# Layer 1 expert weights: partitions that hold neighbouring rows

## The chip, the cores and the metric

The kernel runs on one core of a Trainium2 chip. The metric is the device time of one execution in microseconds (us). The engines are PE (TensorE matmul; its weight loads are shown as PEld), DVE (VectorE), ACT (ScalarE), POOL (GpSimd) and SP (SyncE, which here only issues transfers); 16 DMA engines move data between HBM and the on-chip memory of 128 partitions.

## The reference, cut to what matters

Two layers of a hybrid model over 256 latent and 256 context tokens, model width 1024, all in float32. Each layer has a mixer (layer 0: SSD heads and a convolution; layer 1: a gated linear recurrence) and behind it a mixture of 16 experts, of which the router gives each token two. The change is in the experts of layer 1, which only the 256 latent tokens pass. With t the tokens (256 x 1024) and combine the weight of each token for each expert:

```
def expert(acc, p):
    wg, wu, wd, gate_col = p           # 1024x512, 1024x512, 512x1024
    y = (silu(t @ wg) * (t @ wu)) @ wd
    return acc + gate_col[:, None] * y, None
out, _ = lax.scan(expert, zeros, (w_gate, w_up, w_down, combine.T))
```

The sum over the 1024 rows of wg and wu, and over the 512 rows of wd, may be taken in any order, so long as each row meets its own channel of the token or of the hidden layer.

## The kernel before, in words

**The weights' stream.** All large weights come through one object, `S` (class Stream, lines 28 to 87). `S.add` enters a transfer in a plan, in the order of use; `fill` (line 62) takes a free buffer from the rings and issues the next transfer of the plan on SP's queue (line 76). `S.done` gives a buffer back and calls `fill`. A buffer is 128 partitions x 8 KB, a transfer 1 MB. The order on SP's queue is thus the plan's, and a transfer starts when the one before it is issued and a buffer is free. Layer 1's experts stand last in the plan (`plan_moe(1)`, line 218): for each expert gate and up of the first 512 rows, gate and up of the second 512 rows, and then the two halves of the down weights of the expert before.

**How a transfer lays out rows.** `rows` (line 206) lays rows r0 to r0 + 128n so that partition p holds rows r0 + p, r0 + 128 + p and so on: `(k p) c -> p k c`. For gate and up n is 4 and a row is 512 f32 (2 KB); for layer 1's down weights n is 2 and a row is 1024 f32 (4 KB). One piece of HBM that follows on is one row.

**The experts of layer 1** (lines 2530 to 2720). The work is written out in order by hand, one expert after the other, with no planner. For a pair of experts `slots1` finds the up to 64 tokens of each, and `gather1` (line 2584) collects their channels with matmuls: the stationary operand is a block of 128 tokens x 128 channels of the normalised tokens `h[t]`, the moving one a one-hot matrix of 128 tokens x 2 x 64 slots, and the result, in PSUM, has 128 channels on the partitions and the slots in the free dimension. `mm` is the helper at line 98 (its call at 99), so all these matmuls have line L99. Block 4 kh + k holds the channels of the rows that weight buffer kh holds in its k-th part. One f32 matmul is two loads and two matmuls in the trace, so a gather (2 x 4 x 2 calls) has 32.

`hidden_half` multiplies the gathered columns with gate and up, side by side in the two halves of the array. `hidden` (line 2606) takes silu and product, turns the 64 x 512 hidden values with four PE transposes (line 2615, data as the stationary operand) so that 128 hidden channels lie on the partitions, and `down1` (line 2621) multiplies these with the down weights. `add1` adds the result back to the tokens' rows in PSUM. Per pass of the loop over e, PE's order is: gate and up of e, down of e - 1, the transposes of e, adding back e - 2, and for every even e the slots and the gather of the next pair. Two experts are one gather.

```
h = [xg_hu[t].rearrange("p (k c) -> p k c", k=8) for t in range(2)]     # L2562
mm(pv[:, k], h[t][:, 4 * kh + k], oh[:, t, 0:n, 0].bitcast(F32), ...)   # L2593
PE.transpose(p[:, CAP * c:CAP * c + CAP], s_[up, 128 * c:128 * c + 128], ident[up, up])   # L2615
```

A branch at line 2731 holds a loop for experts with more than 64 tokens; its own loads are at line 2743.

Of the kernel before, what the change touches and what calls it, by code (L numbers as in the profile page):

```python
# [6 lines left out]
F32 = mybir.dt.float32  # L7
# [9 lines left out]
D = 1024  # L17
# [72 lines left out]
def build(tc, I, out):  # L90
# [4 lines left out]
    PE, DV, SC, GP, SY = nc.tensor, nc.vector, nc.scalar, nc.gpsimd, nc.sync  # L95


    def mm(o, l, r, start=True, stop=True):
        PE.matmul(o, l, r, start=start, stop=stop, skip_group_check=True)  # L99
# [17 lines left out]
    def ps_tr():  # L117
        return ps.tile([128, 512], F32, name="tr", tag="tr", bufs=2)

    def ps_y(shape=(128, 512)):  # L120
        return ps.tile(list(shape), F32, name="y", tag="y", bufs=2)
# [82 lines left out]
    S = Stream(nc)  # L204

    def rows(ap, r0, n, c0, w):
        return ap[r0:r0 + 128 * n, c0:c0 + w].rearrange("(k p) c -> p k c", p=128)

    w_in = I["ab_w_in"][0]
    w_out = I["ab_w_out"][0]  # L210
    hw_in = I["hg_w_in"][0]
# [6 lines left out]
    def plan_moe(l):  # L218
        def down(e):
            for hf in range(2):  # L220
                if l:
                    S.add(("d", l, e, hf), rows(I["moe_w_down"][l, e], 256 * hf, 2, 0, D))
                else:
                    S.add(("d", l, e, hf), rows(I["moe_w_down"][l, e], 0, 4, 512 * hf, 512))
        gu = (("g", "moe_w_gate"), ("u", "moe_w_up"))
        for e in range(NEXP):
            for (n, w), kh in [(x, kh) for kh in range(2) for x in gu] if l else [(x, kh) for x in gu for kh in range(2)]:
                S.add((n, l, e, kh), rows(I[w][l, e], 512 * kh, 4, 0, 512))
            if e:
                down(e - 1)  # L230
        down(NEXP - 1)
# [39 lines left out]
    for b in MOD_ROUTE:  # L271
        plan_mod(1, b)
    plan_moe(0)
    for b in MOD_TAIL:
        plan_mod(1, b)
# [17 lines left out]
    for kh in range(2):  # L293
        for hf in range(2):
            S.add(("ho", hf, kh), rows(hw_out, 512 * kh, 4, 512 * hf, 512))
    plan_moe(1)


# [17 lines left out]
    def unit(pool, name, dt=F32):  # L316

        return pool.tile([128, 2048], dt, name=name, tag=name, bufs=1)
# [57 lines left out]
    def mask(name, op, dt=F32):  # L376
        t = const.tile([128, 128], dt, name=name)
        DV.tensor_scalar(t, jp, 0.0, None, op0=op)
        return t

    ident = mask("ident", ALU.is_equal)
# [96 lines left out]
    class Pieces:  # L478
# [26 lines left out]
        def next(self, keep=False):  # L505

            if not keep:
                self.release()
            self.ahead()
            v, r, b = self.ready.pop(self.pos)  # L510
            self.pos += 1
            self.held.append((r, b))
            return v
# [57 lines left out]
    def quarter(u, i):  # L571

        return u[i // 4][:, 512 * (i % 4):512 * (i % 4) + 512]
# [632 lines left out]
    oh, ol = ([quarter(uo, 8 * j + c) for c in range(8)] for j in range(2))  # L1206
# [1193 lines left out]
    for hb in range(2):  # L2400
        lb = LB.main()
        for j, i in enumerate((4, 2)):
            p = PS.main()
# [26 lines left out]
        for d in range(2):  # L2430
            if d:
                q = QS.main()
# [50 lines left out]
    xg_hu = [hu[3][:, D * t:D * t + D] for t in range(2)]  # L2483
# [18 lines left out]
    for kh in range(2):  # L2502
# [3 lines left out]
        for hf in range(2):  # L2506
            for i in range(2):
                wh, wl = next_piece()
                for a in range(2):
                    for q in range(2):  # L2510
                        k = 4 * kh + 2 * i + q
                        l, r = tail["oth"][:, k, 128 * a:128 * a + 128], tail["otl"][:, k, 128 * a:128 * a + 128]
# [11 lines left out]
    T, CAP = 256, 64  # L2524
# [3 lines left out]
    def mt(name, shape, bufs=1, dt=F32):  # L2528
        return mp.tile(list(shape), dt, name=name, tag=name, bufs=bufs)

    def pair_tile():
        return mt("oneh", [128, 2, 2, 2, CAP], 2, F32R)

    def which(oh, rank):

        for i in range(rank.shape[2]):
            DV.tensor_tensor(oh[:, :, i], bc(iot[:, None, None, 0:CAP], [128, 2, 2, CAP]),
                             bc(rank[:, :, i][:, :, None, None], [128, 2, 2, CAP]), op=ALU.is_equal)
# [20 lines left out]
    pc = route([0, 0], mt, bt, rv, vb, False, ps_tr,  # L2559
               (lambda: row_half(0), lambda: row_half(1), lambda: which(OH[0], rv[:, :, 0, 0:2].bitcast(F32))))  # L2560
    S.ring([rows_s], last=moe_last[1])
    h = [xg_hu[t].rearrange("p (k c) -> p k c", k=8) for t in range(2)]  # L2562
    gh, itok = (hp.tile([128, n], F32, name=m, tag=m, bufs=1) for m, n in (("masksr", 512), ("masks", T)))
    GP.iota(itok, pattern=[[1, T]], base=0, channel_multiplier=0, allow_small_or_imprecise_dtypes=True)
    fg = [wp.tile([128, 512], F32, name="fg", tag="tmp", bufs=2) for _ in range(2)]
# [4 lines left out]
    def slots1(oh, cols):  # L2570

        n = len(cols)
        p = ps_tr()
        for i, col in enumerate(cols):
            for t in range(2):
                mm(p[:, 4 * i:4 * i + 4], oh[:, t, i].rearrange("p c l -> p (c l)"), col[:, t], t == 0, t == 1)
        yield
        tw = mt("tw", [128, 2, 2], 4)
        pv = p[:, 0:4 * n].rearrange("p (i c) -> p i c", i=n)
        DV.tensor_scalar(tw[:, 0:n, 0], pv[:, :, 1], BIG, None, op0=ALU.add)  # L2580
        DV.tensor_reduce(tw[:, 0:n, 1], pv[:, :, 2:4], axis=AX.X, op=ALU.add)
        yield tw

    def gather1(oh, n):

        n_x[0] += 1
        x = xy[:, 1024 * (n_x[0] % 2):1024 * (n_x[0] % 2) + 8 * n * CAP].rearrange("p (k i l) -> p k i l", k=8, i=n)
        for kh in range(2):
            p = ps_tr()
            pv = p[:, 0:4 * n * CAP].rearrange("p (k i l) -> p k i l", k=4, i=n)  # L2590
            for k in range(4):
                for t in range(2):
                    mm(pv[:, k], h[t][:, 4 * kh + k], oh[:, t, 0:n, 0].bitcast(F32), k == 0 and t == 0, t == 1)  # L2593
                if k % 2:
                    yield
            SC.activation(x[:, 4 * kh:4 * kh + 4], pv, AF.Copy)
            yield None if kh else x

    def hidden_half(acc, x, wg, wu, kh):

        for k in range(4):
            for c, w in enumerate((wg, wu)):
                mm(acc[CAP * c:CAP * c + CAP], x[:, 4 * kh + k], w[:, k], kh == 0 and k == 0, kh == 1 and k == 3)
            yield

    def hidden(acc):

        s_, up = mt("sg", [128, 512]), slice(CAP, 2 * CAP)
        SC.activation(s_[up], acc[0:CAP], AF.Silu)  # L2609
        DV.tensor_tensor(s_[up], s_[up], acc[up], op=ALU.mult)  # L2610
        for _ in range(4):
            yield
        p = ps_tr()
        for c in range(4):
            PE.transpose(p[:, CAP * c:CAP * c + CAP], s_[up, 128 * c:128 * c + 128], ident[up, up])  # L2615
        yield
        a = mt("hT", [128, 4, CAP], 2)
        SC.activation(a.rearrange("p c l -> p (c l)"), p[:, 0:4 * CAP], AF.Copy)
        yield a
# [23 lines left out]
    def add1(z, back, last):  # L2643

        for t in range(2):
            for hf in range(2):
                mm(res[t][hf], back[:, 128 * t:128 * t + 128], z[hf], False, last)
# [19 lines left out]
    def gather_of(q):  # L2667
        v = last_of(gather1(OH[q], 2))
        XT1.update({2 * q + i: v[:, :, i] for i in range(2)})
# [61 lines left out]
    with tc.If(most > CAP):  # L2731
        rvD = dram.tile([128, 8, 16], F32, name="rvD1")
        SY.dma_start(rvD[:, :, :], rv.bitcast(F32).rearrange("p t i e -> p (t i) e"))
        wov = [unit(hw, f"hu{i}") for i in (7, 8)]
        with tc.For_i(0, NEXP, 1) as e:
            col, colr = mt("col", [128, 2, 4]), mt("colr", [128, 2, 4], dt=F32R)
            SY.dma_start(col.rearrange("p t (i o) -> p (t i) o", o=1), rvD[:, :, bass.ds(e, 1)])
            DV.tensor_copy(colr, col)

            def weights(w, r0, n):  # L2740
                nw[0] += 1
                t = wov[nw[0] % 2].rearrange("p (k c) -> p k c", k=n)
                SY.dma_start(t, I[w][1][bass.ds(e, 1), r0:r0 + 128 * n, :].rearrange("o (k p) c -> p (o k) c", p=128))
                return t

            for b in range(1, T // CAP):
                DV.tensor_scalar(col[:, :, 0], col[:, :, 0], -float(CAP), None, op0=ALU.add)
                oh = pair_tile()
                which(oh, col[:, :, 0:1])
                *_, tw = slots1(oh, [colr])  # L2750
                tw = tw[:, 0]
                x = next(v for v in list(gather1(oh, 1)) if v is not None)[:, :, 0]
                acc = ps_y()
                for kh in range(2):
                    for _ in hidden_half(acc, x, *(weights(w, 512 * kh, 4) for w in ("moe_w_gate", "moe_w_up")), kh):
                        pass
                *_, a = hidden(acc)
                *_, v = down1(a, [weights("moe_w_down", 256 * kh, 2) for kh in range(2)], tw)
                add1(*v, True)
# [13 lines left out]
    for t in range(2):  # L2773
        for hf in range(2):
            o = XL[:, t][:, 512 * hf:512 * hf + 512]
# [41 lines left out]
```

## Time and profile before

| | |
|---|---|
| median of 3 runs | 1571.52 us (1570.26 to 1576.47) |
| profiled execution | 1573.54 us, span 1571.7 us |
| PE busy | 1402.3 us, 89% |
| weight loads (PEld) | 940.1 us, 60% |
| DVE, ACT, POOL busy | 59%, 48%, 41% |
| mean granted TensorE clock | 0.953 of full speed |
| DMA over the span | 337.67 MB, 215 GB/s, 181,687 packets |

How to read it: the page divides the span into 40 slices, gives the costliest groups of instructions, and follows the chain of work that ended last back from the end. Shares over the span are means over stages with different limits, so the stage of layer 1's experts is read by itself, with windows, the chain in order of time, the waits, and groups by line and shape. In a group the operation stands as out<-in, then its shapes, its count, its busy time in us and the mean ns of one. For a matmul `tr<-oneh,hu 128*128 128x128`, the first input is the moving operand, the second the stationary one, and 128*128 is the stationary operand's size. Loads and matmuls overlap, so the busy time of a group is less than count times mean.

### The profile page before, as it was taken

How to read it: one execution, taken by the hardware profiler on the slowest of the kernel's cores; microseconds unless marked ns; L12 is line 12 of the kernel's file. 1: busy time of each engine (PE TensorE's matmuls, PEld its weight loads, DVE VectorE, ACT ScalarE, POOL GpSimd, SP SyncE). 2: the span in 40 equal slices, each digit the busy share in tenths (PEclk: the TensorE clock that was granted, in tenths of full speed). 3: DMA queues.
4: the chain of work that ended last, by engine and by line, in shares of the span. 5: the costliest groups of instructions: out<-in, count | busy, mean ns of one | idle time of the engine just before them, and what ended most of it. 6: DMA issues, size and time to landing. Idle time of an engine off the chain costs nothing. (4 is left out here: it accounts for less than half of the span.)

```text
span 1571.7 us, 19457 instructions
## 1 busy us (share of the span) xinstructions
PE 1402.3 (89%) x7312; PEld 940.1 (60%) x7312; DVE 931.9 (59%) x1254; ACT 755.9 (48%) x1269; POOL 641.1 (41%) x398
## 2 busy tenths in 40 slices
PE   5999989796688988899999994899999888999996
PEld 2677755454476665576666761678787665444442
DVE  2675540899396466789999883544554555222223
ACT  4453435363535534588877882644453553121222
POOL 4343324787855374356668551342243223000000
PEclk8999999898899999899999997899999999999998
DMA  9256443553023154899999995422122568999994
GB/s 330 86 148 155 120 119 134 161 188 107 0 75 140 54 216 158 302 368 373 373 372 335 343 371 220 156 81 81 54 71 66 208 220 320 340 395 393 395 393 172
DMA packets 181687, 337.67 MB, mean 215 GB/s; under 512 B 7513, under 2 KB 44641, under 8 KB 181072
## 3 DMA queue, kind: packets, MB, share of 16 engines
q1 hardware_dynamic: 176112, 323.69, 59.4%
q0 software_dynamic: 4208, 8.90, 1.9%
q10 hardware_dynamic: 1264, 3.73, 0.6%
q8 instruction: 61, 1.00, 0.3%
q14 instruction: 42, 0.34, 0.1%
HBM read 329.12 MB, written 11.37 MB: 217 GB/s over the span
## 5 line engine op out<-in xcount | busy, mean ns | idle before, releaser
L475 POOL TENSOR_TENSOR wb<-wring,wb 128x1024 fp32r<-128x1024 f32 x68 | 170.3, 2507 | 277.3 <-ACT wb L474 234.4
L99 PE MATMUL acc<-hh,wb 128*128 128x512 f32 x640 | 207.3, 400 | 4.0 <-ACT wb L474 2.1
L474 ACT ACTIVATE wb<-wring 128x1024 fp32r<-128x1024 f32 x90 | 94.8, 1058 | 106.0 <-PE acc L99 58.9
L99 PEld LDWEIGHTS acc<-hh,wb 128*128 128x128 f32 x640 | 119.2, 188 | 39.1 <-issue 6.0
L99 PE MATMUL acc<-wb,um 128*96 128x512 f32 (+1 forms) x480 | 122.8, 402 | 5.9 <-DVE wb L475 2.9
L99 PE MATMUL acc<-hl,wb 128*128 128x512 f32 x320 | 126.8, 396 | 0.3 <-DVE hl L600 0.2
L717 DVE SCALAR_TENSOR_TENSOR ca<-u,pcol,ca 128x572 f32<-128x572 f32 x87 | 109.7, 1319 | 0.0
L99 PEld LDWEIGHTS acc<-wb,um 128*96 128x96 f32 (+1 forms) x480 | 79.1, 169 | 38.8 <-DVE wb L475 6.2
L2778 POOL TENSOR_TENSOR xl<-xl,fg 128x512 f32<-128x512 f32 x1 | 1.3, 1264 | 242.4 <-ACT xl L2777 242.4
L99 PE MATMUL y<-hu,hu 128*64 128x512 f32 (+2 forms) x296 | 85.6, 522 | 2.9 <-DVE hu L2161 2.8
L2610 DVE TENSOR_TENSOR sg<-sg,y 64x512 f32<-64x512 f32 x16 | 11.1, 692 | 120.6 <-ACT sg L2609 120.6
L475 POOL TENSOR_TENSOR um<-wring,um 128x1024 fp32r<-128x1024 f32 x17 | 53.8, 3162 | 55.4 <-ACT um L474 53.1
L99 PE MATMUL acc<-um,um 128*96 128x512 f32 (+2 forms) x272 | 69.3, 395 | 2.8 <-POOL um L475 2.8
L99 PEld LDWEIGHTS acc<-hl,wb 128*128 128x128 f32 x320 | 60.1, 188 | 15.2 <-DVE hl L600 1.6
L475 DVE TENSOR_TENSOR wb<-uo,wb 128x1024 fp32r<-128x1024 f32 x32 | 60.6, 1927 | 9.7 <-ACT wb L474 9.3
L99 PE MATMUL acc<-uo,um 128*96 128x512 f32 (+1 forms) x240 | 62.9, 400 | 0.0
L475 POOL TENSOR_TENSOR um<-uo,um 128x1024 fp32r<-128x1024 f32 x18 | 50.3, 2796 | 26.7 <-ACT um L474 26.6
L869 DVE SCALAR_TENSOR_TENSOR xa<-xin,pcol,xa 128x514 f32<-128x514 f32 x64 | 58.7, 918 | 2.3
L2609 ACT ACTIVATE sg<-y 64x512 f32<-64x512 f32 x16 | 9.4, 589 | 96.9 <-PE y L99 96.9
L99 PEld LDWEIGHTS y<-hu,hu 128*64 128x64 f32 (+2 forms) x296 | 32.0, 152 | 38.1 <-issue 33.1
L99 PEld LDWEIGHTS acc<-um,um 128*96 128x96 f32 (+1 forms) x272 | 43.7, 177 | 17.9 <-POOL um L475 5.6
L99 PE MATMUL acc<-wb,hxh 128*128 128x512 f32 x160 | 52.7, 411 | 0.0
(666 smaller groups left out, 3503.6 us busy)
## 6 DMA issues: line engine op xcount, KB each, us to landing
wring<-in_mod_w_dram SPq DMA_DIRECT2D x32, 1024.0 KB, 5.4
uo<-in_moe_w_down_dram SPq DMA_DIRECT2D x19, 1024.0 KB, 14.9
wring<-in_moe_w_gate_dram SPq DMA_DIRECT2D x16, 1024.0 KB, 14.2
hu<-in_moe_w_gate_dram SPq DMA_DIRECT2D x16, 1024.0 KB, 13.7
uo<-in_moe_w_up_dram SPq DMA_DIRECT2D x13, 1024.0 KB, 10.0
wring<-in_moe_w_up_dram SPq DMA_DIRECT2D x13, 1024.0 KB, 9.1
wring<-in_hg_w_in_dram SPq DMA_DIRECT2D x13, 1024.0 KB, 5.1
hu<-in_moe_w_down_dram SPq DMA_DIRECT2D x13, 1024.0 KB, 12.7
```

Source lines behind the costliest of these rows:

```text
L99: PE.matmul(o, l, r, start=start, stop=stop, skip_group_check=True)
L474: SC.activation(hv, w, AF.Copy)
L475: eng.tensor_tensor(lv, w, hv.bitcast(F32), op=ALU.subtract)
L717: DV.scalar_tensor_tensor(a, x, w, a, op0=ALU.mult, op1=ALU.add)
L869: DV.scalar_tensor_tensor(a[:, 0:514], x[:, k:k + 514], par("sc_w", 16 * k + i), a[:, 0:514], op0=ALU.mult, op1=ALU.add)
L2609: SC.activation(s_[up], acc[0:CAP], AF.Silu)
L2610: DV.tensor_tensor(s_[up], s_[up], acc[up], op=ALU.mult)
L2778: GP.tensor_tensor(o, o, fg[hf], op=ALU.mult)
```

## The change

Layer 1's expert weights are laid out with `rows_p` in place of `rows`: `(p k) c -> p k c`, so that partition p holds rows r0 + np to r0 + np + n - 1, which follow each other in HBM: 4 rows of 2 KB for gate and up, 2 rows of 4 KB for down, 8 KB in both cases. The k-th part of a buffer now belongs to rows k, k + n, k + 2n and so on. The operands that meet these rows are taken to match: the gather's stationary operand is every fourth f32 of 512 channels, and the transposes' one every second f32 of 256 hidden channels. Layer 0's experts and all other weights stay as they are.

```
+    def rows_p(ap, r0, n):
+        return ap[r0:r0 + 128 * n, :].rearrange("(p k) c -> p k c", k=n)
...
-                    S.add(("d", l, e, hf), rows(I["moe_w_down"][l, e], 256 * hf, 2, 0, D))
+                    S.add(("d", l, e, hf), rows_p(I["moe_w_down"][l, e], 256 * hf, 2))
...
-                S.add((n, l, e, kh), rows(I[w][l, e], 512 * kh, 4, 0, 512))
+                S.add((n, l, e, kh), rows_p(I[w][l, e], 512 * kh, 4) if l else rows(I[w][l, e], 512 * kh, 4, 0, 512))
...
-    h = [xg_hu[t].rearrange("p (k c) -> p k c", k=8) for t in range(2)]
+    h = [xg_hu[t].rearrange("p (h q k) -> p h k q", h=2, k=4) for t in range(2)]
...
-                    mm(pv[:, k], h[t][:, 4 * kh + k], oh[:, t, 0:n, 0].bitcast(F32), k == 0 and t == 0, t == 1)
+                    mm(pv[:, k], h[t][:, kh, k], oh[:, t, 0:n, 0].bitcast(F32), k == 0 and t == 0, t == 1)
...
+        sv = s_.rearrange("p (h q k) -> p h k q", h=2, k=2)
...
-            PE.transpose(p[:, CAP * c:CAP * c + CAP], s_[up, 128 * c:128 * c + 128], ident[up, up])
+            PE.transpose(p[:, CAP * c:CAP * c + CAP], sv[up, c // 2, c % 2], ident[up, up])
...
-                SY.dma_start(t, I[w][1][bass.ds(e, 1), r0:r0 + 128 * n, :].rearrange("o (k p) c -> p (o k) c", p=128))
+                SY.dma_start(t, I[w][1][bass.ds(e, 1), r0:r0 + 128 * n, :].rearrange("o (p k) c -> p (o k) c", k=n))
```

## Rows read from the trace of the kernel before

**Rows 1.** Windows: busy us (instructions) of PE, PEld, DVE, ACT, POOL, clock, DMA share, GB/s.

```profile
1373.10:1401.30 28.20, 28.20 (x151) 12.99 (x152) 7.24 (x14) 5.66 (x10) 0.00 (x0) 1.00 1.04 395
...
1538.80:1557.50 18.70, 17.23 (x78) 6.23 (x78) 7.37 (x12) 5.45 (x9) 0.00 (x0) 1.00 0.41 166
```

**Rows 2.** Chain that ended last, in order of time: start us, us, what.

```profile
1327.25 4.17 PE tr L99 x36
...
1368.91 4.23 PE tr L99 x36
1373.14 7.02 PE y L99 x32
1380.16 3.43 PE tr L99 x16
1383.59 0.39 PE tr L2615 x4
1383.98 1.13 PE acc L99 x4
...
1545.80 3.46 PE tr L99 x16
```

**Rows 3.** Waits of PE's weight loads, 1332 to 1557 us: total us, times, longest.

```profile
PEld y L99 <- DMA rows_s<-in_moe_w_gate_dram: 0.3, 1, 0.3
PEld y L99 <- DMA rows_s<-in_moe_w_down_dram: 0.3, 1, 0.3
PEld y L99 <- DMA xc<-in_moe_w_down_dram: 0.3, 1, 0.3
```

**Rows 4.** DMA from 1350 to 1550 us: rate in 40 bins, queue's packets, MB, share.

```profile
GB/s 246 389 405 390 387 405 392 386 401 395 387 396 399 388 392 406 385 388 409 388 387 406 389 388 401 394 387 394 402 387 391 404 386 390 408 387 385 406 407 115
...
q1 hardware_dynamic: 31888, 76.55, 101.3%
```

**Rows 5.** Groups by line and shape: busy us, mean ns, idle before; last row whole span.

```profile
L99 PEld LDWEIGHTS tr<-oneh,hu 128*128 128x128 f32 x256 | 29.7, 192 | 2.3 <-issue 1.5
...
L2615 PEld LDWEIGHTS tr<-ident,sg 64*128 64x128 f32 x64 | 5.2, 138 | 14.5 <-issue 12.2 <-DVE sg L2610 2.3
...
L99 PEld LDWEIGHTS tr<-rv,oneh 128*128 128x128 f32 x32 | 4.6, 190 | 0.6
...
L99 PE MATMUL tr<-oneh,hu 128*128 128x128 f32 x256 | 31.8, 279 | 1.4 <-DVE q L1614 1.4
...
L99 PEld LDWEIGHTS y<-uo,ones 128*32 128x32 f32 x16 | 1.1, 108 | 1.6 <-issue 1.6
```

**Rows 6.** Groups of DVE and ACT; the L2062 rows from 980 and 1002 us on.

```profile
L1564 DVE TENSOR_REDUCE wn<-bt 128x32 f32<-128x128 f32 x1 | 0.3, 281 | 0.0
...
L383 DVE TENSOR_REDUCE ident<-ident 128x32 f32<-128x128 f32 x1 | 0.4, 368 | 0.0
...
L2062 ACT ACTIVATE tmp<-tr,modc,A 128x256 f32<-128x256 f32 x4 | 2.0, 560 | 1.4 <-PE tr L2054 1.0 <-DVE hcl L2066 0.4
...
L2062 ACT ACTIVATE tmp<-tr,modc,A 128x256 f32<-128x256 f32 x4 | 2.8, 798 | 1.2 <-DVE hxl L2066 1.2
```

**Rows 7.** Last transfers: issue (start us, us), first use by PE, landing time (us, last).

```profile
1529.57 2.22 SPq L76 DMA_DIRECT2D rows_s<-in_moe_w_down_dram x1
...
1531.88 1.25 SPq L76 DMA_DIRECT2D hu<-in_moe_w_down_dram x1
...
1550.68 1.94 PE L99 MATMUL tr<-rows_s,hT 128*64 128x512 f32 x8
...
1552.45 1.89 PE L99 MATMUL tr<-hu,hT 128*64 128x512 f32 x8
...
hu<-in_moe_w_down_dram SPq DMA_DIRECT2D x10, 1024.0 KB, 13.9
...
rows_s<-in_moe_w_down_dram SPq DMA_DIRECT2D x3, 1024.0 KB, 14.0
```

**Rows 8.** Windows, columns as in rows 1: a stretch with a lower granted clock.

```profile
600.00:700.00 100.00, 85.91 (x427) 59.18 (x427) 78.34 (x141) 60.20 (x78) 46.64 (x35) 0.90 0.82 291
```

## The prediction

> **What bounds the kernel now.** The page says that PE is busy for 89% of the span and the 16 DMA engines for 59%; both are averages over stages, so I went to the stage that the change touches: the expert loop of layer 1, from about 1327 us to 1557 us. Four views, in this order.
>
> First the windows by stretch [rows 1]. [...] Two resources are saturated at once, so this view can't say which one sets the time.
>
> Then the chain of waits [rows 2]. From 1327 us to 1549 us it is made of PE pieces one behind the other, and the same pieces have the same length each time: 7.02 us of gate and up products for an expert, 3.43 us of down products, 0.39 us for the four transposes, 1.13 us for adding back, and for each pair of experts once 4.2 us for slots and gather. 2 x (7.02 + 3.43 + 0.39 + 1.13) + 4.22 = 28.2 us, which is the window. A loop that waited for transfers would show pieces of uneven length, or DMA pieces between them.
>
> Then who waited for whom in the loop [rows 3]. PE's weight loads waited for a DMA three times, 0.3 us each: 0.9 us in all. Everything else that PE's loads wait for is their own order of issue.
>
> Last the DMA view [rows 4]: 76.55 MB in 200 us, in 31,888 packets (2,400 B each on average, a mixture of 2 KB for gate and up and 4 KB for down), and the rate in bins of 5 us goes up and down between 385 and 409 GB/s. A pair of experts needs 12 transfers of 1 MB, 12.58 MB, in 28.2 us, 446 GB/s; the transfers don't keep that rate, they live off a lead that they won before 1332 us. So the transfers are close to PE, but behind it only by their lead. PE bounds this stage.
>
> **The change part by part.**
>
> **Pieces of 8 KB.** The same 96 transfers of 1 MB, issued by the same SP queue in the same order into the same buffers; no instruction and no wait is added or moved. The 64 gate and up transfers go from 512 pieces to 128, the 32 down transfers from 256 to 128. What 8 KB pieces do to the rate no row shows. From the bins of 5 us [rows 4]: at the best bin's 409 GB/s the 76.55 MB would take 187 us instead of 200, 13 us sooner; at the worst bin's 385 GB/s about as long as now. On the path I cost the gain at zero, up to 0.9 us [rows 3], because PE's own chain hides it. The loss has a cover too: the last two transfers are issued at 1529.57 and 1531.88 us and land 14.0 and 13.9 us later (medians of their groups), at 1543.6 and 1545.8 us; PE reads them at 1550.68 and 1552.45 us [rows 7]. The smaller slack is 6.6 us, 3% of the loop, so transfers that were over 3% slower would begin to cost, and a PE that gets slower only widens that.
>
> **The gather.** It computes the same products, but its stationary operand was 128 f32 next to each other and is now every fourth one, a step of 16 bytes. There are 8 gathers of 32 loads and 32 matmuls (256 of each), and all 8 are on the chain [rows 2, 5]. Is a longer load hidden by the matmuls? No: the 256 loads take 29.7 us busy, 116 ns each, and the matmuls 31.8 us, 124 ns; the 32 loads for the slots stand before matmuls of only 4 columns and still take 144 ns each [rows 5]. The load sets the pace of this piece already, and each nanosecond that it gains goes to the chain.
>
> What a step of 16 bytes costs a weight load no row of PE shows, for none of its loads here steps. The nearest rows are of other engines [rows 6]. On DVE a reduction of 128 elements to 32 takes 281 ns where it reads neighbours (L1564) and 368 ns where it reads with a step of 32 f32 (L383): (368 - 281) / 128 = 0.68 ns more per element. On ACT the same activation of 256 elements takes 560 ns for the context, written to neighbours, and 798 ns for the latents, written with a step of 4 f32, which is just our 16 bytes: (798 - 560) / 256 = 0.93 ns more. For a load of 128 columns that is 87 to 119 ns, for 256 of them 22.3 to 30.5 us. The other end is nothing, and below nothing I see no reason for: no element less is read. I take the middle of the two rows, 0.80 ns, 102 ns a load, **26.2 us**, because a load of 128 columns takes 192 ns and one of 32 columns 108 ns, so 0.88 ns per column [rows 5], in the same band as both engines (their 256 or 128 elements at about 1 ns), and both of them nearly double.
>
> [...]
>
> **The transposes.** 64 of them (four for each expert) now load every second f32 of 128, a step of 8 bytes [rows 2, 5]. If that cost as much as the ACT row it would be 0.93 x 128 x 64 = 7.6 us; the lower end is nothing. The step is half that of the row, so I halve it, 3.8 us, and take off what the group has spare: its four loads take 0.32 us (5.2 us over 16) of the 0.39 us that the chain shows, 0.07 us x 16 = 1.1 us. I take **2.7 us**. [...]
>
> **The spare loop** for more than 64 tokens on an expert changes its loads in the same way; no row of its lines is in the trace, so it isn't entered: 0.
>
> **Sum.** -0 (transfers) + 26.2 + 2.7 = 28.9 us. The profiled execution took 1573.54 us (span 1571.7 and 1.84 around it) and would take 1602.4; the median of the runs shown, 1571.52, is 2.0 us below it, so I forecast 1571.5 + 28.9 = **1600.4 us**. DVE and ACT have over 20 us of each pair free [rows 1], so nothing of theirs is late next; SP waits longer for the buffers that PE frees, and the three waits for DMA go.
>
> **The rivals.**
>
> **The step is free.** For it: the transposes' loads of 128 columns take 138 ns, where the gather's take 192 [rows 5]. With the 108 ns of 32 columns (80 ns fixed at 0.88 ns per column) that is 0.45 ns per column against 0.88: PE's port gives twice what the gather's loads ask of it, and a slower read may fit into that half. Against it: both rows of other engines. It decides if a load that steps still takes 192 ns. Then only the 0.9 us can move: 1571.5, from 1569 to 1574. [...]
>
> **The transfers do set the loop (faster).** For it: a share of 1.04 and a need of 446 GB/s against 395 [rows 1, 4]. Against it: 0.9 us of waits and 6.6 us of slack at the end [rows 3, 7]. If PE's even pieces hid a wait and the step were free, the 13 us of the best bin would come off: 1558.5. It decides where the pieces of 7.02 us get shorter.
>
> **The clock falls (slower still).** With loads twice as long PE's matmuls pause half of the time for some 7 us in each pair, and elsewhere PE's clock is below full where it pauses: 0.90 from 600 to 700 us at 86% busy [rows 8]. At that level the loop's 225 us would take 25 us more: 1625. Against it: the clock is 1.00 throughout the loop now, and between two gathers stand 24 us of dense products.
>
> **The pieces stay 2 KB**, if the rows that follow each other are still issued one by one. Since the transfers are covered, the time would be that of the forecast or of the free step.
>
> **How the numbers follow.** Forecast 0.60, free step 0.30, clock 0.06, transfers 0.04. The measurement can tell 0.5% (7.9 us) from no change: below 1563.7 is faster, above 1579.4 slower. Faster 0.05 (the transfers, and a bit for what I don't see), same 0.30, slower 0.65 (forecast and clock). The forecast's own range is 22.3 us to 30.5 + 7.6 us more, 1594 to 1609. The free step alone holds more than 2 in 10, so the range goes down to its lower end: 1569 to 1608.
>
> **What would show it.** Right: the gather's 32 loads at about 290 ns mean instead of 192 and its piece on the chain at 7.5 us instead of 4.2; the transposes' group at 0.45 to 0.6 us; the pieces of 7.02 and 3.43 us unchanged; packets near 8 KB, the DMA share below 1 in the loop. Wrong: gather pieces still of 4.2 us (free step), pieces of 7.02 us that change (transfers), a granted clock below 1.00 in the loop. A loop over 30 us longer with gathers of 7.5 us would mean that a cost sits where I have none.

## The result, and the profile after

The changed kernel takes 1607.06 us (median of 4 runs, 1605.13 to 1607.96) against 1570.89 us before: slower, ratio 1.0225 with a 95% interval of 1.0204 to 1.0245. The forecast was 1600.4 us in a range of 1569 to 1608; it was right on the sign and on the place, and 6.7 us short in size, so the time lies 0.9 us below the top of the range.

The profiled executions have spans of 1605.8 and 1571.7 us, 34.1 us apart. The chain of waits after, in order of time (start us, us, what), answers to [rows 2]:

```profile
1327.85 8.06 PE tr L99 x36
...
1377.98 7.91 PE tr L99 x36
1385.89 7.02 PE y L99 x32
1392.91 3.43 PE tr L99 x16
1396.34 0.62 PE tr L2622 x4
1396.96 1.13 PE acc L99 x4
...
1583.20 16.22 issue
```

What was 4.2 us for slots and gather is 7.9, what was 0.39 us for four transposes is 0.62, and the pieces of gate and up (7.02), down (3.43) and adding back (1.13) have not moved. From the start of the first gather to the end of this chain are 255.4 us, where before they were 222.0 (1327.25 to 1549.28): 33.3 of the 34.1 us are in the loop. The sum of the pieces says the same: the eight pieces with a gather go from 33.8 to 63.7 us (+29.9), 15 groups of transposes gain 0.23 us each (+3.5). One gather, the second, takes 8.21 us (4.31 before); the granted clock was 0.79 on average there (1346.5 to 1354.7 us) and 1.00 in the pairs behind it.

The groups by line and shape (busy us, mean ns, idle before) show which half of PE's work got longer; they answer to [rows 5]:

```profile
L99 PEld LDWEIGHTS tr<-oneh,hu 128*128 128x128 f32 x256 | 60.4, 329 | 1.5 <-issue 1.5
...
L2622 PEld LDWEIGHTS tr<-ident,sg 64*128 64x128 f32 x64 | 8.8, 208 | 14.5 <-issue 12.2 <-DVE sg L2615 2.3
L99 PEld LDWEIGHTS tr<-rv,oneh 128*128 128x128 f32 x32 | 4.7, 190 | 0.6
```

The gather's load takes 60.4 / 256 = 236 ns busy where it took 116. The slots' load beside it, of the same size and without a step, is as before (4.7 us).

The DMA view from 1350 to 1580 us (answers to [rows 4]) shows that the transfers did what the change says:

```profile
GB/s 177 113 425 425 425 415 388 368 420 417 429 416 255 417 420 426 426 385 266 429 420 425 419 261 415 427 416 426 415 191 412 420 426 427 386 189 4 0 0 0
DMA packets 10677, 77.74 MB, mean 338 GB/s; under 512 B 1196, under 2 KB 1196, under 8 KB 1196
```

A third of the packets, nine in ten of 8 KB, and up to 429 GB/s where the bins of before go from 385 to 409. The bins at 113 to 266 hold pauses in which SP waits for PE to free a buffer (from 1350 to 1560 us such waits come to 175.1 us, the longest 13.1). None of it reaches the path: the last transfer is issued at 1551.90 us and lands about 12 us later (the median of its group is 12.2), and PE reads it at 1586.6 us; the slack that was 6.6 us [rows 7] is over 20.

### The profile page after: what moved, and what is told of

The parts are those of the page before. It is cut to its first block, busy times and chain, and to the rows that moved or that the text cites. A ratio compares the mean times of both kernels' runs of the same rounds, so it can differ in the third digit from the quotient of the medians.

```text
span 1605.8 us, 19457 instructions
## 1 busy us (share of the span) xinstructions
PE 1438.6 (90%) x7312; PEld 976.5 (61%) x7312; DVE 934.2 (58%) x1254; ACT 755.9 (47%) x1269; POOL 638.1 (40%) x398
## 5 line engine op out<-in xcount | busy, mean ns | idle before, releaser
L99 PE MATMUL tr<-oneh,hu 128*128 128x128 f32 x256 | 61.7, 402 | 1.4 <-DVE q L1618 1.4
L99 PEld LDWEIGHTS tr<-oneh,hu 128*128 128x128 f32 x256 | 60.4, 329 | 1.5 <-issue 1.5
```

## The experiments

Two theories stood at first: that the step of PE's stationary operand costs the time, and that the larger pieces disturb PE's reads. The first two kernels take the change apart, the next three vary the step, and then come the places where the two halves of the change could be worth something. Beside each time stands the length of the loop, from the start of the first gather to the end of PE's chain; it is steadier than the whole time, since runs of the kernel before alone went from 1566 to 1577 us.

**The pieces alone.** The changed transfers, the operands contiguous again.

```
-    h = [xg_hu[t].rearrange("p (h q k) -> p h k q", h=2, k=4) for t in range(2)]
+    h = [xg_hu[t].rearrange("p (h k q) -> p h k q", h=2, k=4) for t in range(2)]
...
-        sv = s_.rearrange("p (h q k) -> p h k q", h=2, k=2)
+        sv = s_.rearrange("p (h k q) -> p h k q", h=2, k=2)
```

> The transfers of the changed kernel (8 KB pieces), with the gather's and the transposes' operands contiguous as before; the channels then meet other rows' weights. Step theory (the cost is the step of PE's stationary operand): the gather's loads are back at 116 ns busy each, its pieces on the chain at 4.2 us, the transposes' groups at 0.39 us, and the time is that of the kernel before, 1571 us, between 1568 and 1574; packets and DMA rate are those of the changed kernel (425 GB/s in the best bins). Contention rival (8 KB pieces disturb PE's reads): the gather pieces stay near 7.9 us and the time near 1605 us. Transfers rival (they set the loop before): 1558 us.

Measured: 1571.45 us, ratio to before 0.9994 (0.9983 to 1.0006), loop 223.7 us. Its chain and its packets:

```profile
1322.53 5.79 PE tr L99 x36
...
1365.83 4.23 PE tr L99 x36
1370.06 7.02 PE y L99 x32
1377.08 3.43 PE tr L99 x16
1380.51 0.40 PE tr L2622 x4
```

```profile
GB/s 423 424 423 423 423 421 413 426 419 421 423 415 423 423 419 426 421 421 416 424 423 416 419 421 421 421 426 418 421 423 418 423 421 419 416 400 57 0 0 0
DMA packets 10431, 75.95 MB, mean 380 GB/s; under 512 B 1168, under 2 KB 1168, under 8 KB 1168
```

The pieces run at some 421 GB/s, the transfers end near 1531 us (the 37th bin of 5 us) instead of 1545.8, and that is worth nothing here: the pieces of PE's chain are as they were, but for the first gather, which takes 5.79 us instead of 4.17 and makes the loop 1.7 us longer; the mean granted clock from 1322 to 1546 us is 0.99 (1.00 before). They also cost nothing, so the disturbance rival falls, and so does the rival by which the transfers set the loop.

**The steps alone.** The transfers of before, the stepped operands.

```
-                S.add((n, l, e, kh), rows_p(I[w][l, e], 512 * kh, 4) if l else rows(I[w][l, e], 512 * kh, 4, 0, 512))
+                S.add((n, l, e, kh), rows(I[w][l, e], 512 * kh, 4, 0, 512))
```

(and the down weights likewise)

> The transfers of the kernel before (2 and 4 KB pieces), with the changed kernel's stepped operands; the channels then meet other rows' weights. Step theory: 1606 us, between 1603 and 1609, gather pieces of 7.9 us and transposes' groups of 0.62 us, as in the changed kernel. Contention rival: near 1571 us, gather pieces of 4.2 us.

Measured: 1604.8 us, ratio 1.0204 (1.0177 to 1.0232), loop 255.4 us, the changed kernel's to a tenth. Its loads:

```profile
L99 PEld LDWEIGHTS tr<-oneh,hu 128*128 128x128 f32 x256 | 60.4, 329 | 1.5 <-issue 1.5
L2622 PEld LDWEIGHTS tr<-ident,sg 64*128 64x128 f32 x64 | 8.8, 209 | 14.5 <-issue 12.2 <-DVE sg L2615 2.3
```

The whole loss is the steps'.

**A gather step of 8 bytes.** Gate and up in pieces of 4 KB, two neighbouring rows on a partition; down and transposes as before. Every channel still meets its own row.

```
+                S.add((n, l, e, kh), I[w][l, e][512 * kh:512 * kh + 512, :].rearrange("(j p k) c -> p j k c", j=2, k=2) if l else ...)
...
+    h = [xg_hu[t].rearrange("p (h j q k) -> p h j k q", h=2, j=2, k=2) for t in range(2)]
```

> Gate and up in pieces of 4 KB (two rows that follow each other on a partition), so that the gather's step is 8 bytes instead of 16; down weights and transposes as before. Shared-fetch theory (two f32 within 16 bytes come with one fetch of 1.8 ns, the 231 ns of the changed kernel over 128 columns): 0.9 ns a column, which is what a contiguous gather load takes already (116 ns), so the gather is back at 4.2 us and the time at 1571 us, between 1568 and 1575. Rival (the extra time grows with the step in proportion, 57 ns for half the step): gather pieces of 6.1 us, 1571 + 256 x 0.057 = 1586 us. Rival (any step costs all): gather pieces of 7.9 us, 1571 + 29.9 = 1601 us.

Measured: 1575.76 us, ratio 1.0017 (0.9998 to 1.0036), loop 223.0 us; six of the eight pieces with a gather at 4.33 us, the first two at 4.36 and 4.51:

```profile
1370.47 4.33 PE tr L103 x36
```

```profile
L103 PEld LDWEIGHTS tr<-oneh,hu 128*128 128x128 f32 x256 | 31.2, 196 | 1.7 <-issue 1.5
```

122 ns a load instead of 116, 0.1 us a piece: a step of 8 bytes is all but free, and one of 16 doubles the load (236 ns). Both rivals fall; the time lies 0.8 us above the range that I had given, and the loop is 1.0 us longer than before.

**A gather step of 32 bytes, a transposes' step of 16.** Transfers of before.

```
+    h = [xg_hu[t].rearrange("p (q k) -> p k q", k=8) for t in range(2)]
...
+        sv = s_.rearrange("p (q k) -> p k q", k=4)
```

> Transfers of the kernel before; the gather's operand steps by 32 bytes and the transposes' one by 16 bytes, so that the channels meet other rows' weights. Shared-fetch theory: 32 bytes cost no more than 16, the gather pieces stay at 7.9 us; the transposes' loads go from about 115 ns at 8 bytes to 231 ns a load, a group of four from 0.62 to about 1.1 us; 1571 + 29.9 + 16 x 0.7 = 1612 us. Rival (extra time in proportion to the step): gather loads at 116 + 2 x 115 = 346 ns, pieces of 11.6 us, some 1640 us.

Measured, in one run: 1598.5 us, loop 256.7 us.

```profile
L99 PEld LDWEIGHTS tr<-oneh,hu 128*128 128x128 f32 x256 | 61.7, 335 | 1.5 <-issue 1.5
L2622 PEld LDWEIGHTS tr<-ident,sg 64*128 64x128 f32 x64 | 8.9, 209 | 14.5 <-issue 12.2 <-DVE sg L2615 2.3
```

The gather half is near what I expected: 241 ns at 32 bytes, 236 at 16, and pieces of 8.06 to 8.09 us from the third on where they were 7.91. The transposes half missed: their loads are no longer at 16 bytes (209 ns) than at 8 (208), and a group stays at 0.62 us. The two kinds of load don't follow one rule.

**Both steps at 12 bytes.**

```
+                    mm(pv[:, k], xg_hu[t][:, 512 * kh + 32 * k:512 * kh + 32 * k + 384].rearrange("p (q k) -> p k q", k=3)[:, 0], ...)
...
+            PE.transpose(p[:, CAP * c:CAP * c + CAP], s_[up, 32 * c:32 * c + 384].rearrange("p (q k) -> p k q", k=3)[:, 0], ident[up, up])
```

> The kernel before with both of PE's stepped operands at 12 bytes (every third f32; the channels meet other rows' weights). For the gather 8 bytes cost nothing and 16 and 32 the same 115 ns a load. If what counts is how many 16-byte stretches 128 elements touch, 12 bytes touch 96 of them against 128: 116 x 96 / 64 = 174 ns a load, pieces of 6.0 us, 1571 + 14.5 + 3.7 = 1589 us. If it is a threshold between 8 and 16 bytes: pieces of 4.2 or of 7.9 us, 1575 or 1605 us. For the transposes, where 8 and 16 bytes both cost 57 ns a load, 57 ns again, groups of 0.62 us.

Measured, in one run: 1588.9 us, loop 241.3 us, six of the eight gather pieces at 6.01 us, the first two at 7.05 and 6.93; the mean granted clock from 1320 to 1565 us was 0.98. The groups over the loop, and last the gather's loads from 1350 us on, behind those two pieces:

```profile
L99 PEld LDWEIGHTS tr<-oneh,hu 128*128 128x128 f32 x256 | 46.7, 271 | 1.5 <-issue 1.5
L2615 PEld LDWEIGHTS tr<-ident,sg 64*128 64x128 f32 x64 | 8.5, 202 | 14.5 <-issue 12.2 <-DVE sg L2610 2.3
...
L99 PEld LDWEIGHTS tr<-oneh,hu 128*128 128x128 f32 x192 | 33.9, 261 | 0.0
```

Over all 256 loads that is 182 ns a load, and 177 from 1350 us on, behind the two longer pieces (174 expected). The five steps together, busy time of one gather load: 116 ns at 4 bytes, 122 at 8, 177 at 12, 236 at 16, 241 at 32. They fit a count of stretches of 16 bytes: 128 elements touch 32, 64, 96, 128 and 128 of them, and from 64 on the times are 1.8 to 1.9 ns a stretch, while at 32 the 116 ns are 0.9 ns per column. That a stretch sets the pace is my estimate from these five times. The transposes' loads don't fit it: at 8 bytes their 128 elements touch 64 stretches, which cost the gather's load 6 ns, and the transposing load takes 208 ns mean where it took 138 for neighbours.

**The kind of load.** The transposes as ordinary f32 matmuls with the identity, step 16 bytes, transfers of before.

```
+        sv = s_.rearrange("p (q k) -> p k q", k=4)
...
-            PE.transpose(p[:, CAP * c:CAP * c + CAP], s_[up, 128 * c:128 * c + 128], ident[up, up])
+            mm(p[:, CAP * c:CAP * c + CAP], sv[up, c], ident[up, up])
```

> The kernel before, but the four transposes of the hidden values are ordinary f32 matmuls with the identity (two loads each, so eight), their stationary operand with a step of 16 bytes (hidden channels meet other rows' weights). Open is why a transposing load pays 57 ns at 8, 12 and 16 bytes alike while the gather's pays 0, 66 and 115. If it is the kind of load: these loads pay as the gather's, 231 ns each, a group of 1.9 us instead of 0.39, 1571 + 16 x 1.5 = 1595 us. If it is that only 64 partitions are read: some 115 ns each, a group of 0.95 us, 1580 us.

Measured, in one run: 1606.1 us, loop 252.4 us; a group of 5.44 - 3.43 = 2.0 us.

```profile
1368.90 5.44 PE tr L99 x24
1374.34 1.13 PE acc L99 x4
1375.47 5.64 PE tr L99 x36
```

```profile
L99 PEld LDWEIGHTS tr<-ident,sg 64*128 64x128 f32 x128 | 31.0, 324 | 14.5 <-issue 12.2 <-DVE sg L2610 2.3
```

31.0 / 128 = 242 ns a load on the same 64 partitions, where the transposing loads at 16 bytes took 8.9 / 64 = 139: it is the kind of load, not the partitions. The time is 11 us over the 1595 expected. The span is 32.5 us longer than before: 15 groups in the loop at 1.62 us more (24.3), 2.1 us behind the chain's end, where the sixteenth stands, and the rest, 6.1, in four pieces that ran slowly. One is the gather piece at 1375.47: 5.64 us instead of 4.23, and the granted clock from 1375.4 to 1381.1 us is 0.70 on average, where it is 1.00 in the 26.0 us ahead and in the 26.9 us behind; it fell just behind groups in which the loads took most of 2 us (8 x 242 ns). Whether these brought it on is not shown: the kernel with the pieces alone, which has no step, took 5.79 us for its first gather, with a mean clock of 0.99 over its loop.

**The step on the moving side.** Gate and up read with 16 bytes of step, all else as before.

```
+                mm(acc[CAP * c:CAP * c + CAP], x[:, 4 * kh + k], w.rearrange("p a b -> p (a b)").rearrange("p (c k) -> p k c", k=4)[:, k], ...)
```

> The kernel before, but the gate and up weights, PE's moving operand, are read with a step of 16 bytes (every fourth f32 of the buffer, so that columns are mixed); all else as before. If the step doubles a moving read as it doubles a load: pieces of 14 us instead of 7.02, 1571 + 16 x 7 = 1683 us. If each moving read takes the 1.8 ns of a stretch and the two matmuls side by side share the port: 32 x 512 x 1.8 = 29.5 us a piece, some 1930 us. Rival (the step only concerns the load side): 1571 us, pieces of 7.02 us.

Measured, in one run: 1692.6 us, loop 342.6 us.

```profile
1394.00 14.58 PE y L99 x31
1408.58 3.44 PE tr L99 x10
```

The pieces go from 7.02 to 14.6 us: 0.91 us for 512 columns of two matmuls side by side, 1.78 ns a column where it was 0.86. The step doubles this moving f32 read as it doubles the gather's load (116 to 236 ns); that the two streams take turns, at 29.5 us a piece, is ruled out.

**The step moved to where the operand is written.** 8 KB pieces throughout, POOL and ACT write the tokens and ACT the hidden values in the order in which PE reads them next to each other. Every channel still meets its own row.

```
+                o = o.rearrange("p (k q) -> p q k", k=4)
...
+        sw = s_.rearrange("p (h k q) -> p h q k", h=2, k=2)
...
+        SC.activation(sw[up], av[0:CAP], AF.Silu)
```

> The 8 KB pieces for gate, up and down, but the step taken off PE: the normalised tokens are written in the order in which the gather reads them next to each other (POOL writes the product with the gain with a step, ACT the shift row), and the hidden values likewise (ACT writes the silu with a step, DVE reads the product's PSUM operand with one). Step theory: PE's gather pieces are back at 4.2 us and the transposes' groups at 0.39 us, the ACT and DVE operations get 0.2 to 0.5 us longer behind 3.43 us of down products, once 0.5 to 1 us shows ahead of the first expert; the time is 1572, between 1568 and 1577. Rival (the step's cost only moves): the writes get onto the chain, 16 experts x 0.5 us and more, 1580 us and above.

Measured: 1574.74 us, ratio to before 1.0011 (0.9995 to 1.0026), loop 222.4 us. ACT's silu takes 1.07 us instead of 0.59, behind 3.43 us of down products for all but the first expert:

```profile
L2623 ACT ACTIVATE sg<-y 64x512 f32<-64x512 f32 x16 | 17.1, 1070 | 97.7 <-PE y L99 97.7
L2633 PEld LDWEIGHTS tr<-ident,sg 64*128 64x128 f32 x64 | 5.2, 138 | 14.9 <-issue 12.2 <-DVE sg L2626 2.8
```

So the layout can be had at no cost that these runs can tell, if an engine with time to spare takes the step. It gains nothing either, as the pieces alone said, so no version here beats the kernel before.

**What the pieces are worth where they aren't covered.** Two kernels gather only the first pair and use its columns for all experts (7 gathers left out), one with the transfers of before, one with 8 KB pieces and contiguous operands.

```
+    X0 = [XT1[i] for i in range(2)]
...
-            gather_of(e // 2 + 1)
+            XT1.update({e + 2 + i: X0[i] for i in range(2)})
```

> The kernel before, but only the first pair of experts is gathered, and its columns serve all 16 (7 gathers left out, so the values are those of the first pair). PE has 7 x 3.9 = 27 us less to do. If the transfers of 2 and 4 KB pieces then set the loop, at 391 GB/s and with an end near 1546 us, only some 6.6 us of it show: 1565, between 1560 and 1570. Rival (PE sets the loop whatever the transfers do): 1571.5 - 27 = 1544.5.

> The same, only the first pair gathered, with 8 KB pieces and contiguous operands on PE (the channels meet other rows' weights). At the 423 GB/s of the run with the pieces alone the transfers end some 16 us sooner, near 1530 us, so that PE's own chain sets most of the loop: 1547, between 1543 and 1553. Against the same kernel with 2 and 4 KB pieces that is the worth of the larger pieces where transfers are not covered: some 18 us. Rival (the pieces are worth nothing): as the other, 1565.

Measured: 1562.91 us (ratio to before 0.9935, 0.9914 to 0.9956; loop 214.8 us) and 1552.13 us (0.9861, 0.9841 to 0.9881; loop 203.5 us). Of the 27 us that PE no longer needs, 7.2 us show in the loop with 2 and 4 KB pieces, 18.5 us with 8 KB. PE's loads in the first of them wait for transfers, in the largest group:

```profile
PEld y L99 <- DMA hu<-in_moe_w_up_dram: 9.0, 4, 2.5
```

where the kernel before has 0.3 us at a time [rows 3]. The larger pieces are worth 10.8 us where the transfers set the time, less than the 18 I expected, because the second kernel still waits for them: 2.4 us in the same row, and 12 us over all rows of PE's loads that wait for a transfer, where the six largest of the first kernel hold 21.3.

## Why the prediction was right

**What bounds the loop.** Confirmed. Of the two that [rows 1] shows full, PE and the DMA engines, PE does: the steps alone give the whole loss, the pieces alone give nothing, and taking work from PE shortens the loop until the transfers stop it.

**Pieces of 8 KB, costed at 0.** Right: 0.9994 (0.9983 to 1.0006). The rate rose more than the best bin of before (bins of 413 to 426 GB/s against 409), and PE's chain hid it all.

**The gather, 26.2 us.** The right mechanism, with a size 3.7 us too small: 29.9 us on the chain, 117 ns a load instead of the 102 assumed. Of the two rows the nearer one was ACT's at the same step of 16 bytes, 0.93 ns per element [rows 6]; on the chain PE's load gained 0.91. I had taken the middle of it and DVE's 0.68, which was at another step. That a write of ACT and a load of PE cost so nearly the same is explained by no run here, so the size came this near partly by luck. The reason given beside it was misread: both rows don't "nearly double" (281 to 368 and 560 to 798 ns), and their whole time is 2.2 ns an element, not about 1; it was the load of PE that doubled, 116 to 236 ns. The argument that a longer load isn't covered by the matmuls held: the loads grew by 30.7 us in busy time and the pieces by 29.9.

**The transposes, 2.7 us.** 3.7 us measured (0.23 x 16), so 1.0 us too small. The reasoning, half the step and half the cost, was wrong although the number came near: 8, 12 and 16 bytes cost a transposing load nearly the same (208, 202 and 209 ns mean, 138 for neighbours).

The sum was 28.9 us; 33.3 us came in the loop of the profiled execution, and 0.8 us of the spans' difference lies outside it (0.6 us before the first gather, 0.3 us behind the chain's end, where the sixteenth group of transposes stands). The medians are 36.2 us apart, 2 us more than the profiled executions, which is within the scatter of the runs.

**The rivals.** The free step fell: a transposing load of neighbours does take less than an ordinary one (81 ns busy against 116), and a step of 8 bytes fits into an ordinary load's time (122 ns), but one of 16 bytes takes 236. The transfers' rival fell with the pieces alone. The clock's rival, 25 us more, did not come: over the changed kernel's loop the clock was 0.99, with a dip to 0.79 in the second gather. Longer pieces also stand in the first gather of the pieces alone (5.79 us, mean clock of the loop 0.99) and in the first two at 12 bytes (7.05 and 6.93 us, 0.98); the kernel whose transposes were ordinary matmuls lost most by slow pieces, 6.1 us. The rival of pieces that stay 2 KB fell too: nine packets in ten are of 8 KB.

**The signs.** The gather's loads came to 329 ns mean (about 290 named) and its pieces to 7.9 us (7.5); the groups of transposes, at 0.62 us, are just past the 0.45 to 0.6 named. The other pieces didn't change, and the DMA share in the loop was 0.79. The loop grew by over 30 us, but the two terms named hold all of it. What didn't come is the end of the waits for DMA: PE's loads waited five times, 1.5 us in all, where it had been three times and 0.9. Two readings of the kernel before were too short: in the window of [rows 3] PE's loads also waited for DVE, 2.3 and 1.7 us, and the chain of [rows 2] holds 1.3 us of ACT and DVE behind the first expert. Neither bears on the sum.

## What to carry to other kernels

Before a layout is changed for the transfers, read whether the transfers end last: a DMA share of 1.04 was no sign of it here, even pieces on PE's chain and waits of 0.3 us were. Then price what the layout does to every reader: an f32 operand of PE read with a step of 16 bytes cost twice its time, as an ordinary matmul's stationary operand (236 ns a load against 116) or as the moving one (14.6 us a piece against 7.02), while 8 bytes cost an ordinary load 6 ns of 116. If a step is needed, let the engine that writes the operand take it, where that engine has time.

## What the runs showed that I had not expected

A transposing f32 load paid 52 to 58 ns of busy time on its 128 columns at 8, 12 and 16 bytes of step alike, while an ordinary one paid 6, 61 and 120. Why the first has no further step up to 16 bytes stays open; other types and bf16 weren't tried. The rate of 1 MB transfers rose with the piece: bins of 385 to 409 GB/s with 2 and 4 KB, 403 to 416 with 4 KB throughout, and 413 to 426 with 8 KB.
